# Bias table, value layout, decay rows and masked products of a hybrid attention/SSD layer rearranged

## The chip, the cores and the metric

One NeuronCore of a Trainium2 chip runs the whole layer as one program. The metric is the device time of an execution in microseconds (us), from the first to the last instruction of the core and what lies around it. The engines are TensorE (PE, with its weight loads as PEld), VectorE (DVE), ScalarE (ACT), GpSimd (POOL) and SyncE (SP). SP issues most of the DMAs, POOL some. Each engine, and each DMA-issuing queue, takes its instructions in order.

## The reference

The layer normalizes and modulates 1024 latent tokens and 256 context tokens of width 1024, projects them, and sends the columns to two groups of heads: eight heads of 2-D neighbourhood attention (a 16 x 64 grid, windows of 8 x 16, with all context keys in the same softmax) and eight heads of a bidirectional Mamba-2 (SSD) scan. An output projection, a gated MLP with a depthwise convolution, and a last RMSNorm follow. The scan in chunks of 128 tokens, for one direction, is

```python
cum = jnp.cumsum(dtc * a.reshape(g, e), axis=2)
seg = cum[:, :, :, None] - cum[:, :, None, :]
decay = jnp.exp(jnp.where(lower, seg, -jnp.inf))
cb = jnp.einsum("bcign,bcjgn->bcijg", cc, bc)
m = cb[..., None] * decay * dtc[:, :, None]
y_diag = jnp.einsum("bcijge,bcjgep->bcigep", m, xc)
...
y = y_f + flip(y_b) + d_skip[:, None] * xs
y = y.reshape(bsz, l, SSD_WIDTH) * jax.nn.silu(z)
```

and a row of the attention adds `rpb` at the window's offsets to the scores, and excludes keys outside the window. All is float32.

## The kernel before, in words

The program runs in stages on one core: norms and modulation; the q/k projections with rotary embedding (lines 278 to 308); the v projection (310 to 328); the SSD inputs with their convolution (508 to 539); the z projection (565 to 579); attention with the rest of the SSD beside it (596 to 781); the output projection; the MLP. Matmuls of the projections are made in three products of high and low parts. q, k, v, z and the summed decay exponents (`cum_d`) go through DRAM scratch tensors and are read back in the layout of the next stage.

**Values.** The v projection runs in two halves `b` of 256 columns. Each half has five units of two token blocks (ten blocks of 128 tokens, the last two context), evacuated into the one buffer of `vt` (L315). Its latent tokens are stored in `v_d` by column blocks `cb` and grid-row parity `r` (L323 to 327), eight stores, and the context in one (L328). `load_v(hp)` (L592) reads one head pair's 18 tiles back, in runs of 128 floats.

**SSD.** `ssd_steps` (L424) is a generator. Its steps are: the two initial states, seven steps of the backward state, then six steps for each of the eight chunks (`ssd_chunk`, L434). They are numbered 0 to 5 here. Step 0 multiplies C and B (`cb`), masks the product for both directions on DVE (`cbm`, L441), loads the decay rows `seg` of both directions, broadcast to 128 partitions, with two DMAs of 512 KB (L446), and subtracts each token's own sum on POOL (L447). Step 1 takes the minimum on DVE and the exp on ACT. Step 2 weights the masks with `dt`: the forward direction on DVE into `mt0`, the backward one on POOL into the buffer of `seg1` (L457), then POOL adds both (L459) and DVE multiplies by the decay (L460). Step 3 makes the products on TensorE (and advances the forward state), steps 4 and 5 gather the parts, multiply with silu(z), and sum the squares on ACT. The pool `sw` has one buffer of each tile.

**Who drives the generator.** The last two units of the SSD inputs take two steps each, the eight z units one each (L577), and each attention step `n` one (L779). Chunk 0 so reaches step 3 in the z stage; its steps 4 and 5 fall on n = 0 and 1, and chunk c (1 to 7) on n = 6c - 4 to 6c + 1. From n = 44 on the generator `out_steps` follows.

**Attention.** 64 steps, each for 128 queries of one head, in groups of eight (one head pair and half of the rows; four column blocks `cb`, two heads `j`). `attn_score` (L616) makes the scores in PSUM, DVE adds the bias table and finds the maximum (L638), ACT takes the exp (L639); `attn_turn`, two steps later, transposes on TensorE and copies on ACT (L650); `attn_out`, three steps later, multiplies with v. The tables, 24 in all, live in two buffers `tabt` (L599 to 608): table m + 1 is loaded at the first use of table m. The zero columns between a table's halves, for the context keys, are set once by POOL. Table 0 is loaded after the z stage, as `at`, the pool that holds `tabt` and `vp`, lies where the z stage's operands were.

**Order.** The program is written in this order, but within it the framework's planner sets the order of instructions of each engine and queue by modelled times, so a load can stand on SP ahead of, or behind, its place in the source. `reuse_waits="tile"` means that a new tile waits for the last use of the tiles whose memory it takes.

Of the kernel before, what the change touches and what calls it, by code (L numbers as in the profile page):

```python
# [17 lines left out]
P = 128  # L18
# [18 lines left out]
def hymba(ctx: ExitStack, tc: tile.TileContext, A):  # L37
# [23 lines left out]
    v_d = dram.tile([18, P, 512], FP, name="v_d")  # L61
# [180 lines left out]
    with ExitStack() as p1:  # L242
# [67 lines left out]
        for b in range(2):  # L310
# [11 lines left out]
            fs = slice(256 * b, 256 * b + 256)  # L322
            for cb in range(4):  # L323
                win = v_d[4 * cb:4 * cb + 4, :, fs].rearrange("g (i r c) f -> r c (g i) f", i=2, r=2)
                for r in range(2):
                    p0 = 64 * r + CB0[cb]
                    sp.dma_start(win[r], vt[p0:p0 + 32, 0:8])
            sp.dma_start(v_d[16:18, :, fs].rearrange("t p f -> p t f"), vt[:, 8:10])  # L328
# [94 lines left out]

    def ssd_steps():  # L424
        init_state(0, hf[0])
        init_state(1, yz[:, 7])
        yield
        for c in range(7, 0, -1):
            advance(1, c, yz[:, c], yz[:, c - 1])
            yield  # L430
        for c in range(8):
            yield from ssd_chunk(c)

    def ssd_chunk(c):  # L434
# [7 lines left out]
        seg = []  # L442
        for d in range(2):
            sg = sw.tile([P, 8, P], FP, tag=f"seg{d}", name=f"seg{d}_{c}")
            r0 = d * 64 + c * 8
            sp.dma_start(sg, cum_d[r0:r0 + 8].partition_broadcast(P))  # L446
            pool.tensor_tensor(sg, sg, cum[:, d, c][:, :, None].to_broadcast([P, 8, P]), OP.subtract)  # L447
            seg.append(sg)
        yield
        dve.tensor_tensor(seg[0], seg[0], seg[1], OP.min)  # L450
        act.activation(seg[0], seg[0], AF.Exp)
        yield
        mt = [sw.tile([P, 8, P], FP, tag="mt0", name=f"mt_{c}"), seg[1]]
        for d in range(2):
            for g in range(2):
                hs4 = slice(4 * g, 4 * g + 4)
                (pool if d else dve).tensor_tensor(mt[d][:, hs4], cbm[:, d, g][:, None, :].to_broadcast([P, 4, P]),  # L457
                                  dtv[:, c, 8 * d + 4 * g:8 * d + 4 * g + 4][:, :, None].to_broadcast([P, 4, P]), OP.mult)
        pool.tensor_tensor(mt[0], mt[0], mt[1], OP.add)  # L459
# [13 lines left out]
        sp.dma_start(yz[:, c], z_d[sl])  # L473
        ya = sw.tile([P, 512], FP, tag="ya", name=f"ya{c}")
# [4 lines left out]
        dve.tensor_tensor(v8(yb), v8(yo[:, 1]), bc64(ecum[:, 1, c]), OP.mult)  # L479
# [722 lines left out]
```

## Time and profile before

| | us |
|---|---|
| median of 3 runs (1397.27 to 1399.0) | 1398.22 |
| the profiled execution | 1403.42 |
| its span, first to last instruction | 1401.7 |

| engine | busy us | share of the span | instructions |
|---|---|---|---|
| PE | 1332.7 | 95% | 7539 |
| DVE | 858.5 | 61% | 1345 |
| ACT | 625.8 | 45% | 1049 |
| POOL | 303.2 | 22% | 295 |

A busy PE is not a PE at its peak: matmuls are pipelined and their ends are modelled. The idle time of an engine counts only where another waits for it. In the rows below, a row of a timeline gives the start and the duration in us, engine, line, operation, tile written and tiles read, shape, and in brackets how long the engine was idle before and what ended that. A row of groups ends with the count, the busy time in us, the mean of one in ns, and the idle time before them with its releasers. A row of windows gives the stretch (A:B), its length, the busy time of PE, PEld, DVE, ACT and POOL with the instructions of each, the granted clock, the DMA share and GB/s. [...]

### The profile page before, as it was taken

To read this page: it belongs to the slowest core of one execution; us is meant where nothing else is said; L and a number is where in the kernel's file an instruction comes from. 1 tells how busy PE (TensorE), PEld (TensorE's weight loads), DVE (VectorE), ACT (ScalarE), POOL (GpSimd) and SP (SyncE) were. 2 spreads that over 40 slices of the span, in tenths; PEclk is the share of its full clock that TensorE was granted. 3 is DMA by queue.
4 is the path that set the end of the run, shared out by engine and by line. 5 is a ranking of instruction groups with operands and counts; after the bars stand their busy time and mean duration, and the time that the engine had idled before them with its cause. 6 is when DMAs were issued, how large, how long until landed. Compare 5 with 4: busy or idle time off the path is not lost.

```text
span 1401.7 us, 20013 instructions
## 1 busy us (share of the span) xinstructions
PE 1332.7 (95%) x7539; PEld 1120.1 (80%) x7539; DVE 858.5 (61%) x1345; ACT 625.8 (45%) x1049; POOL 303.2 (22%) x295
## 2 busy tenths in 40 slices
PE   4999999999899999999989999999999999999996
PEld 2788998889877887777886888888888877887985
DVE  5684246742367766548877555666556584668664
ACT  5441224332155558536556444454445453455441
POOL 0010000024667752000222222221222102110120
PEclk9999999999999999999999999999999999999998
DMA  9564675521697687333857677766677677686782
GB/s 370 215 166 121 164 239 198 183 91 60 191 253 195 201 229 252 112 136 120 188 129 186 158 177 168 166 157 159 144 174 175 178 261 188 174 240 169 193 210 74
DMA packets 118160, 251.02 MB, mean 179 GB/s; under 512 B 11944, under 2 KB 37288, under 8 KB 116784
## 3 DMA queue, kind: packets, MB, share of 16 engines
q1 hardware_dynamic: 92576, 197.58, 43.9%
q0 software_dynamic: 25488, 52.18, 19.9%
q8 instruction: 59, 0.97, 0.3%
q14 instruction: 37, 0.30, 0.1%
HBM read 212.16 MB, written 37.55 MB: 178 GB/s over the span
## 4 chain that ended last, share of the span: by engine, by line
PE 77%; DMA 8%; DVE 5%; ACT 4%; POOL 3%; issue 3%; SPq 0%; DVEq 0%; POOLq 0%; ACTq 0%
PE u L871 27%; PE pd L90 10%; PE fu_qk L90 6%; PE fu_x L90 6%; PE tu_v L90 4%; PE oc L90 3%; PE tu_z L90 2%; PE pm L1037 2%; PE av L666 2%; DMA seg<-cum_d 2%; PE os L90 2%; PE oa L90 1%; PE pt L648 1%; PE fu_c L90 1%; DMA as<-in_w_up 1%
## 5 line engine op out<-in xcount | busy, mean ns | idle before, releaser
L871 PE MATMUL u<-op,whu 128*128 128x512 f32 (+1 forms) x760 | 227.0, 382 | 4.5 <-ACT yz L889 2.8
L871 PEld LDWEIGHTS u<-op,whu 128*128 128x128 f32 x760 | 139.4, 189 | 36.0 <-ACT yz L889 3.7
L871 PE MATMUL u<-op,wlu 128*128 128x512 f32 (+1 forms) x380 | 144.0, 380 | 0.0
L844 POOL DMA_DIRECT2D as<-in_w_up x69 | 65.9, 984 | 354.8 <-DMA as<-in_w_up 145.7
L863 ACT ACTIVATE whu<-as 128x512 fp32r<-128x512 f32 x115 | 67.6, 625 | 166.7 <-PE u L871 158.8
L871 PE MATMUL u<-opx,whu 128*128 128x512 f32 (+1 forms) x384 | 111.2, 381 | 4.1 <-ACT whu L863 3.6
L864 DVE TENSOR_TENSOR wlu<-as,whu 128x512 fp32r<-128x512 f32 x115 | 75.9, 685 | 24.7 <-ACT whu L863 24.6
L871 PEld LDWEIGHTS u<-opx,whu 128*128 128x128 f32 x384 | 70.5, 190 | 20.2 <-ACT whu L863 5.2
L90 PE MATMUL pd<-opx,wh_dn 128*128 128x512 f32 x256 | 81.5, 399 | 3.4 <-ACT wh_dn L79 3.3
L871 PEld LDWEIGHTS u<-op,wlu 128*128 128x128 f32 x380 | 71.7, 189 | 15.0
L894 DVE TENSOR_TENSOR xa<-u,yz 128x512 f32<-128x512 f32 (+1 forms) x24 | 15.5, 645 | 94.1 <-PE u L871 94.1
L871 PE MATMUL u<-opx,wlu 128*128 128x512 f32 (+1 forms) x192 | 72.0, 378 | 0.0
L639 ACT ACTIVATE pr<-pr,mx 128x640 f32<-128x640 f32 x64 | 52.8, 825 | 40.1 <-DVE mx L638 40.0
L638 DVE CUSTOM_DVE_ANT_0 pr<-s,tabt 128x640 f32<-128x640 f32 x64 | 51.9, 817 | 21.3 <-PE s L628 15.4
L666 PE MATMUL av<-pts,vp 128*64 128x128 f32 x640 | 56.6, 289 | 5.0 <-ACT pts L650 5.0
L90 PEld LDWEIGHTS pd<-opx,wh_dn 128*128 128x128 f32 x256 | 47.7, 189 | 16.7 <-ACT wh_dn L79 5.4
L851 POOL DMA_DIRECT2D yz<-in_w_up x46 | 52.2, 1158 | 33.9 <-ACT yz L850 30.4
L650 ACT ACTIVATE pts<-pt 128x640 f32<-128x640 f32 x64 | 43.9, 695 | 33.1 <-PE pt L648 20.7
L871 PE MATMUL u<-opz,whu 128*128 128x512 f32 (+1 forms) x192 | 56.3, 376 | 1.2 <-ACT yz L886 1.2
L666 PEld LDWEIGHTS av<-pts,vp 128*64 128x64 f32 x640 | 41.5, 142 | 17.8 <-ACT pts L650 8.6
L648 PE MATMUL pt<-cst,pr 128*128 128x128 f32 x320 | 49.2, 285 | 5.9 <-ACT pr L639 3.2
L627 PE MATMUL s<-k,q 128*128 128x384 f32 x128 | 49.8, 409 | 1.5 <-DVE mx L638 1.3
(641 smaller groups left out, 3571.1 us busy)
## 6 DMA issues: line engine op xcount, KB each, us to landing
as<-in_w_up SPq DMA_DIRECT2D x69, 256.0 KB, 4.0
as<-in_w_up POOLq DMA_DIRECT2D x69, 256.0 KB, 3.7
yz<-in_ada_wt SPq DMA_DIRECT2D x32, 512.0 KB, 4.4
ws_dn<-in_w_down SPq DMA_DIRECT2D x32, 448.0 KB, 4.2
as<-in_w_up SPq DMA_DIRECT2D x23, 512.0 KB, 5.5
yz<-in_w_up POOLq DMA_DIRECT2D x46, 256.0 KB, 5.6
g_d<-xa POOLq DMA_DIRECT2D x22, 512.0 KB, 4.8
tabt<-in_tab SPq DMA_DIRECT2D x48, 192.0 KB, 4.7
```

The source lines that it names most:

```text
L90: pe.matmul(out[:, t0:t1], st(a, k), mv(b, k, t0, t1), start=k == 0 and p == 0, stop=k == kend - 1 and p == 2, **kw)
L627: pe.matmul(ps[:, loc0:loc0 + 384], qs, kl, start=a == 0, stop=a == 1)
L638: dve.tensor_tensor_reduce(pr, ps[:, lo:lo + 640], tabt[m % 2][:, 384 * j:384 * j + 640], -1.0, BIG, OP.add, OP.min, mx)
L639: act.activation(pr, pr, AF.Exp, bias=mx, scale=-1.0, accum_out=sm[:, n % 8:n % 8 + 1])
L648: pe.transpose(pt[:, i * P:(i + 1) * P], pr[:, i * P:(i + 1) * P], ident)
L650: act.activation(pts, pt[:, 0:640], AF.Copy)
L666: pe.matmul(av[64 * j:64 * j + 64, cb], vt, pp[j][:, i * P:(i + 1) * P], start=i == 0, stop=i == 4, skip_group_check=True)
L844: pool.dma_start(t, d, accum_op=OP.add)
L851: pool.dma_start(t, d, accum_op=OP.add)
L863: act.activation(h, src, AF.Copy)
L864: dve.tensor_tensor(l, src, f32(h), OP.subtract)
L871: mm = pe.matmul(ps[:, t0:t1], aops[n, o][a][:, k], bops[o][b][:, k, t0:t1], start=first and o < 5 and (t0 == 0 or n == 2), stop=end, skip ...
```

## The change

- **First table.** Table 0 goes into the first 1024 columns of `ctm`, a tile of the context tokens that is free once the initial states are made; its loads and the zeroing stand in the first step of the second half of the z stage. The two `tabt` buffers take the other tables in turn.
- **Values.** `v_d` is laid out by head pair and partition, so that a head pair's load has one run of 18 x 128 floats in each partition. The stores of a half become 32 of 64 KB for the latent tokens and two for the context; the 32 of the second half are issued by POOL.
- **Decay rows.** Even chunks keep their two decay tiles in `sw`, odd chunks have theirs in a second pool `swx`, opened beside `at` when the z stage is over. The load for chunk c + 1 stands at step 0 of chunk c, its subtraction at step 5 of chunk c (chunk 0: load ahead of the initial states, subtraction at its own step 0; chunk 1: load at step 4 of chunk 0).
- **Masked products.** ACT multiplies the backward mask with `dt`, head by head, into `mt0`; DVE then multiplies the forward mask with `dt` and adds, head by head, in place. POOL's products and its sum are gone.
- **Moved.** The square of a chunk stands at step 1 of the next one, the last one after all chunks; POOL's sum of `yb` and `xd` moves from step 5 to step 4.

```diff
-    v_d = dram.tile([18, P, 512], FP, name="v_d")
+    v_d = dram.tile([4, P, 18, P], FP, name="v_d")
...
-            fs = slice(256 * b, 256 * b + 256)
-            for cb in range(4):
-                win = v_d[4 * cb:4 * cb + 4, :, fs].rearrange("g (i r c) f -> r c (g i) f", i=2, r=2)
-                for r in range(2):
-                    p0 = 64 * r + CB0[cb]
-                    sp.dma_start(win[r], vt[p0:p0 + 32, 0:8])
-            sp.dma_start(v_d[16:18, :, fs].rearrange("t p f -> p t f"), vt[:, 8:10])
+            for hp in range(2):
+                v = vt[:, :, P * hp:P * hp + P]
+                vd = v_d[2 * b + hp]
+                for cb in range(4):
+                    win = vd[:, 4 * cb:4 * cb + 4].rearrange("(i r c) g f -> r i c g f", i=2, r=2)
+                    for r in range(2):
+                        p0 = 64 * r + CB0[cb]
+                        for i in range(2):
+                            (pool if b else sp).dma_start(win[r, i], v[p0:p0 + 32, i:8:2])
+                sp.dma_start(vd[:, 16:18], v[:, 8:10])
...
+    def seg_load(c):
+        segs[c] = []
+        for d in range(2):
+            sg = swx[c % 2].tile([P, 8, P], FP, tag=f"seg{d}", name=f"seg{d}_{c}")
+            r0 = d * 64 + c * 8
+            sp.dma_start(sg, cum_d[r0:r0 + 8].partition_broadcast(P))
+            segs[c].append(sg)
+
+    def seg_less(c):
+        for d in range(2):
+            pool.tensor_tensor(segs[c][d], segs[c][d], cum[:, d, c][:, :, None].to_broadcast([P, 8, P]), OP.subtract)
+
+    def square(c):
+        yb = sw.tile([P, 512], FP, tag="yb", name=f"sq{c}")
+        act.activation(yb, yz[:, c], AF.Square, accum_out=ssq[:, c:c + 1])
...
     def ssd_steps():
+        seg_load(0)
         init_state(0, hf[0])
...
         for c in range(8):
             yield from ssd_chunk(c)
+        square(7)
...
-        seg = []
-        for d in range(2):
-            sg = sw.tile([P, 8, P], FP, tag=f"seg{d}", name=f"seg{d}_{c}")
-            r0 = d * 64 + c * 8
-            sp.dma_start(sg, cum_d[r0:r0 + 8].partition_broadcast(P))
-            pool.tensor_tensor(sg, sg, cum[:, d, c][:, :, None].to_broadcast([P, 8, P]), OP.subtract)
-            seg.append(sg)
+        if c == 0:
+            seg_less(0)
+        elif c < 7:
+            seg_load(c + 1)
+        seg = segs.pop(c)
         yield
+        if c:
+            square(c - 1)
         dve.tensor_tensor(seg[0], seg[0], seg[1], OP.min)
         act.activation(seg[0], seg[0], AF.Exp)
         yield
-        mt = [sw.tile([P, 8, P], FP, tag="mt0", name=f"mt_{c}"), seg[1]]
-        for d in range(2):
-            for g in range(2):
-                hs4 = slice(4 * g, 4 * g + 4)
-                (pool if d else dve).tensor_tensor(mt[d][:, hs4], cbm[:, d, g][:, None, :].to_broadcast([P, 4, P]),
-                                  dtv[:, c, 8 * d + 4 * g:8 * d + 4 * g + 4][:, :, None].to_broadcast([P, 4, P]), OP.mult)
-        pool.tensor_tensor(mt[0], mt[0], mt[1], OP.add)
+        mt = [sw.tile([P, 8, P], FP, tag="mt0", name=f"mt_{c}")]
+        for h in range(8):
+            act.activation(mt[0][:, h], cbm[:, 1, h // 4], AF.Copy, scale=dtv[:, c, 8 + h:9 + h])
+        for h in range(8):
+            dve.scalar_tensor_tensor(mt[0][:, h], cbm[:, 0, h // 4], dtv[:, c, h:h + 1], mt[0][:, h], OP.mult, OP.add)
         dve.tensor_tensor(mt[0], mt[0], seg[0], OP.mult)
...
         sp.dma_start(yz[:, c], z_d[sl])
+        if c == 0:
+            seg_load(1)
...
+        pool.tensor_tensor(yb, yb, xd, OP.add)
         yield
+        if c < 7:
+            seg_less(c + 1)
         dve.tensor_tensor(ya, ya, yd, OP.add)
-        pool.tensor_tensor(yb, yb, xd, OP.add)
         dve.tensor_tensor(ya, ya, yb, OP.add)
         pool.tensor_tensor(yz[:, c], ya, yz[:, c], OP.mult)
-        act.activation(yb, yz[:, c], AF.Square, accum_out=ssq[:, c:c + 1])
...
+    tabt = [ctm]
+    table = lambda m: tabt[1 + m % 2 if m else 0]
...
                 if b and not qks:
+                    pool.memset(ctm[:, 384:640], 0.0)
+                    for j in range(2):
+                        load_tab(0, j)
                     load_qk(0)
...
-        sp.dma_start(vps[hp], v_d[:, :, P * hp:P * hp + P].rearrange("t p f -> p t f"))
+        sp.dma_start(vps[hp], v_d[hp])
```

## Rows read from the trace of the kernel before

**Rows 1.** Chain of waits from 350 to 640 us: shares by line

```profile
by line: PE av L666 10.0%; DMA seg<-cum_d 9.7%; PE os L90 8.5%; PE oa L90 7.0%; PE pt L648 6.8%; PE s L627 5.5%; issue 5.4%; POOL mt L459 3.2%; PE s L628 2.8%; POOL seg L447 2.6%; DMA tabt<-in_tab 2.6%; DVE pr L638 2.5%; PE tu_z L90 2.4%; P
```

**Rows 2.** Windows over chunks 1 to 7: stretch, length, busy by engine, clock, DMA

```profile
377.96:401.99 24.03, 19.34 (x132) 16.44 (x133) 13.43 (x29) 10.17 (x22) 13.90 (x10) 0.86 1.04 292
401.99:422.76 20.77, 18.48 (x152) 15.57 (x152) 17.41 (x25) 11.43 (x23) 16.62 (x11) 1.00 0.74 208
422.76:440.33 17.57, 17.25 (x140) 14.35 (x139) 14.38 (x27) 11.82 (x24) 10.08 (x8) 1.00 0.92 241
440.33:465.43 25.10, 22.65 (x165) 19.50 (x164) 15.66 (x26) 10.32 (x22) 19.43 (x14) 0.86 0.74 232
465.43:483.90 18.47, 18.47 (x155) 15.81 (x154) 15.21 (x27) 11.93 (x25) 13.54 (x9) 1.00 0.42 118
483.90:508.99 25.09, 22.39 (x160) 19.41 (x159) 14.53 (x26) 11.08 (x22) 16.07 (x11) 0.86 0.90 242
508.99:527.38 18.39, 17.67 (x148) 14.88 (x147) 13.81 (x26) 11.47 (x25) 8.29 (x6) 1.00 0.78 198
```

**Rows 3.** Timeline of DVE: the minimum of the decay tiles, chunks 2 to 7

```profile
402.30 2.29 DVE L450 TENSOR_TENSOR seg<-seg,seg 128x1024 f32<-128x1024 f32 x1
...
420.24 2.28 DVE L450 TENSOR_TENSOR seg<-seg,seg 128x1024 f32<-128x1024 f32 x1 [1.31 <-POOL seg L447]
...
445.80 2.05 DVE L450 TENSOR_TENSOR seg<-seg,seg 128x1024 f32<-128x1024 f32 x1 [3.73 <-POOL seg L447]
...
470.30 1.23 DVE L450 TENSOR_TENSOR seg<-seg,seg 128x1024 f32<-128x1024 f32 x1 [0.56 <-POOL seg L447]
...
492.21 1.22 DVE L450 TENSOR_TENSOR seg<-seg,seg 128x1024 f32<-128x1024 f32 x1 [2.68 <-POOL seg L447]
...
513.39 1.21 DVE L450 TENSOR_TENSOR seg<-seg,seg 128x1024 f32<-128x1024 f32 x1
```

**Rows 4.** Chain of waits at chunk 4, in order of time: start, length, what

```profile
430.58 2.38 POOL mt L459
432.98 7.90 DMA seg<-cum_d
441.01 1.90 POOL seg L447
```

**Rows 5.** Timeline of DVE at the start of attention: the first score operation

```profile
383.19 0.82 DVE L638 CUSTOM_DVE_ANT_0 pr<-s,tabt 128x640 f32<-128x640 f32 x1 [2.63 <-DMA tabt<-in_tab]
```

**Rows 6.** Groups by line and shape: masked products, and the nearest small operations

```profile
L457 POOL TENSOR_TENSOR seg<-cbm,dtv 128x512 f32<-128x512 f32 x16 | 20.1, 1273 | 7.4 <-DVE seg L450 3.7 <-DVE cbm L441 3.6
L459 POOL TENSOR_TENSOR mt<-mt,seg 128x1024 f32<-128x1024 f32 x8 | 19.3, 2410 | 1.2 <-DVE mt L457 0.7
...
L457 DVE TENSOR_TENSOR mt<-cbm,dtv 128x512 f32<-128x512 f32 x12 | 13.1, 1131 | 0.0
...
L356 DVE SCALAR_TENSOR_TENSOR dta<-dtv,na 128x160 f32<-128x160 f32 x1 | 0.3, 326 | 0.0
...
L347 ACT ACTIVATE dt<-dt 128x160 f32<-128x160 f32 x1 | 0.3, 338 | 0.0
...
L639 ACT ACTIVATE pr<-pr,mx 128x640 f32<-128x640 f32 x36 | 29.7, 825 | 21.6 <-DVE mx L638 21.6
L650 ACT ACTIVATE pts<-pt 128x640 f32<-128x640 f32 x37 | 25.5, 695 | 20.8 <-PE pt L648 15.8 <-PE av L666 4.9
```

**Rows 7.** v: stores on SP; the projection in the chain; DMA issues; POOL's own

```profile
166.73 6.44 SPq L327 DMA_DIRECT2D v_d<-vt  x8
...
142.76 58.29 PE tu_v L90 x480
...
v_d<-vt SPq DMA_DIRECT2D x18, 256.0 KB, 4.0
vp<-v_d SPq DMA_DIRECT2D x4, 1152.0 KB, 9.4
...
L905 POOL DMA_DIRECT2D g_d<-xa x22 | 15.4, 698 | 79.1 <-DVE xa L904 79.1
```

More of the change, by code (lines that the diff above doesn't have):

```diff
@@ L422, in advance @@
         dve.tensor_tensor(dst, tmp, ps, OP.add)
+    segs = {}
+    def seg_load(c):
[11 more added lines that the diff above has]
+        act.activation(yb, yz[:, c], AF.Square, accum_out=ssq[:, c:c + 1])
     def ssd_steps():
+        seg_load(0)
         init_state(0, hf[0])
@@ L518, in hymba @@
             sw = open_sw()
+            swx = [sw]
             hf = [sw.tile([P, 512], FP, name=f"hf{i}") for i in range(2)]
@@ L541, in hymba, with load_tab @@
     qks = {}
+    tabt = [ctm]
+    table = lambda m: tabt[1 + m % 2 if m else 0]
+    def load_tab(m, j):
+        if m < 24:
+            c = 640 * j
+            sp.dma_start(table(m)[:, c:c + 384], A["tab"][2 * (m // 6) + j, m % 6])
     def load_qk(g):
@@ L585, in hymba @@
     at = pb.enter_context(tc.tile_pool(name="at", reuse_waits="tile", bufs=2))
+    sx = ExitStack()
+    swx.append(sx.enter_context(tc.tile_pool(name="swx", reuse_waits="tile", bufs=1)))
     bigp = pb.enter_context(tc.tile_pool(name="bigp", reuse_waits="tile", bufs=3, space=PSUM))
@@ L593, in load_v @@
         vps[hp] = at.tile([P, 18, P], FP, tag="vp", name=f"vp{hp}", bufs=2)
-        sp.dma_start(vps[hp], v_d[:, :, P * hp:P * hp + P].rearrange("t p f -> p t f"))
+        sp.dma_start(vps[hp], v_d[hp])
+    tabt += [at.tile([P, 1024], FP, name=f"tabt{i}", bufs=1) for i in range(2)]
+    for t in tabt[1:]:
+        pool.memset(t[:, 384:640], 0.0)
     load_v(0)
@@ L598, in hymba @@
     sp.dma_start(selh, A["selh"])
-    tabt = []
-    for i in range(2):
-        t = at.tile([P, 1024], FP, name=f"tabt{i}", bufs=1)
-        pool.memset(t[:, 384:640], 0.0)
-        tabt.append(t)
-    def load_tab(m, j):
-        if m < 24:
-            c = 640 * j
-            sp.dma_start(tabt[m % 2][:, c:c + 384], A["tab"][2 * (m // 6) + j, m % 6])
-    for j in range(2):
-        load_tab(0, j)
     steps = [(hp, rb, cb, j) for hp in range(4) for rb in range(2) for cb in range(4) for j in range(2)]
@@ L637, in attn_score @@
         mx = at.tile([P, 1], FP, tag="mx", name=f"mx{n}", bufs=4)
-        dve.tensor_tensor_reduce(pr, ps[:, lo:lo + 640], tabt[m % 2][:, 384 * j:384 * j + 640], -1.0, BIG, OP.add, OP.min, mx)
+        dve.tensor_tensor_reduce(pr, ps[:, lo:lo + 640], table(m)[:, 384 * j:384 * j + 640], -1.0, BIG, OP.add, OP.min, mx)
         act.activation(pr, pr, AF.Exp, bias=mx, scale=-1.0, accum_out=sm[:, n % 8:n % 8 + 1])
@@ L708, in out_steps @@
         nonlocal xa
+        sx.close()
         sd.close()
```

## The prediction

> **What bounds the kernel now.** I first read the chain of waits over the stretch that the diff touches, from the end of the z projection to the first output projection. TensorE's lines fill most of it, but one transfer stands second: the load of the decay rows, `seg<-cum_d`, with 9.7% [rows 1]. TensorE should never wait for a 512 KB load whose contents were known long before, so the next view cuts the stretch into the seven SSD chunks that run beside the attention scores. Each chunk is six generator steps, one step per attention step, so the cuts stand at the first score matmul of every sixth attention step. The chunks take 24.03, 20.77, 17.57, 25.10, 18.47, 25.09 and 18.39 us, 149.42 us in all, for the same work but for what falls on a cut [rows 2]. Three are slow, three quick, and chunk 2 lies between. The slow ones (1, 4, 6) are also those whose granted clock is 0.86 instead of 1.00.
>
> What tells slow from quick is on DVE: before the minimum of a chunk's two decay tiles it sat idle for POOL's subtraction, not at all in chunk 2, 1.31 us in 3, 3.73 in 4, 0.56 in 5, 2.68 in 6, not at all in 7 [rows 3]. So a wait over 2.5 us makes a slow chunk, one up to 1.3 us a quick one. The size fits: against the mean of the three quick ones, (17.57 + 18.47 + 18.39) / 3 = 18.14 us, chunks 4 and 6 take 7.0 us more, of which the waits are 3.7 and 2.7, and a clock of 0.86 over 25.1 us loses (1 - 0.86) x 25.1 = 3.5 us of full clock: 7.2 and 6.2. The low clock comes in no chunk without such a wait (chunk 1 has the start's, below). Chunk 2's 2.6 us have another cause: the same minimum takes 1.2 us in some chunks and 2.3 in others [rows 3], and chunk 2 has DVE busy for 17.41 us against 13.8 to 15.2 in the quick ones, with POOL at its densest (16.62 of 20.77, 80%) [rows 2]; I read this as DVE slowed by POOL's work.
>
> Why the rows come late shows in the chain at chunk 4: POOL's sum of the masked products ends, the load runs 7.90 us, then the subtraction starts [rows 4]. The products of chunk c are built in the buffer of its second decay tile, and there is one buffer of each tile, so chunk c+1's rows cannot be loaded before chunk c's products are finished. Products, load, subtraction, minimum, exp, products form a loop through four engines, and behind the minimum DVE's other work (the sums that free the one PSUM bank of the SSD products) waits in order.
>
> The start has a stall of its own: DVE's first score operation waits 2.63 us for the first bias table and starts at 383.19 [rows 5], behind the z stage.
>
> **The change part by part.** *Decay rows a chunk ahead* (second pair of buffers, load at step 0 of the chunk before, subtraction at its step 5). It removes nothing but the dependence: 14 loads and 14 subtractions are still made. A load now has five steps, 5 x 17.57 / 6 = 14.6 us at the quickest chunk's pace, against 7.90 us for the late one. With no wait left, and the 5 us that POOL loses below gone from beside DVE, I give chunks 2 to 7 the 18.14 us of the quick ones: 6 x 18.14 = 108.9 against 125.4 now, **-16.5 us**. On SP the load moves ahead of the tables and q/k loads of five steps; its buffer was freed four steps before, so it holds nothing up. What is late next is DVE, busy 14 to 15 us of a quick chunk [rows 2].
>
> *First table in a free buffer.* The two loads move into the z stage, where TensorE is fed by other data, so they cost nothing: no engine waits for them before the z stage has ended. The 2.63 us wait goes. Chunk 1 is 24.03 - 18.14 = 5.9 us over a quick one; part of the rest is the low clock, which should not come if the pause is shorter. Against it, chunk 1's own rows now go to memory that is free only when the z stage has ended, and land later than before; their slack is the products of that chunk. Bounds: 0 and 5.9; I take **-4 us**.
>
> *Products head by head.* Removed per chunk: on POOL two products of 1.27 us and a sum of 2.41 us, 4.95 us; on DVE two products of 1.13 us, 2.26 us. Added: eight ACTIVATEs of 128x128 and eight SCALAR_TENSOR_TENSORs of 128x128 [rows 6]. Neither shape, with a per-partition scalar from SBUF, is in the trace. For DVE the nearest is 128x160 from SBUF in 326 ns; 8 x 0.326 = 2.6 us is an upper end, as the new ones are 32 columns shorter, and I take them as equal to the 2.26 that goes. For ACT the nearest is 128x160 in 338 ns, 8 x 0.338 = 2.7 us; the score exp, with a scalar from SBUF, takes 825 ns at 640 columns against 695 for the copy without, and with those 130 ns on each the upper end is 3.7 us. I take 2.7, the row of nearly the same shape. ACT is busy 11.5 to 11.9 us of the quick chunks [rows 2], so about 14.4 of 18.1. I take the pair at **0**: the cover is ACT's idle 6 us per chunk. If it covers nothing, 7 x 2.7 = 18.9 us come back; on the other side, a freer POOL, and DVE beside it, could give up to (18.14 - 17.1) x 6 = 6 us more (17.1 is worked out below).
>
> [...] The trace's own nearest row is the 338 ns for 160 columns [rows 6]. [...]
>
> *Values in long runs.* The load of v has 1152 KB, landing in 9.4 us [rows 7]; with one run per partition I expect less, but it is taken at 0, as the first product that needs it comes behind the scores. The stores come in smaller pieces: per half 32 of 64 KB and two for the context instead of 8 of 256 KB and one. Before, eight took 6.44 us to issue, 0.81 us each, on SP; the new ones, a quarter of the bytes, lie between 0.2 (by bytes) and 0.81 (by count). At 0.4 us (twice the price by bytes), 34 take 13.6 us. The first half's end at 166.7 + 13.6 + 4.0 us of landing = 184 [rows 7]. The tile `vt` has one buffer, so the next half's first copy, due when its unit ends at 142.76 + 6 x 5.83 = 177.7 [rows 7], waits some 6 us; three PSUM buffers of 5.83 us hide that until about 190. So **0**; at 0.81 us it would be 34 x 0.81 = 27.5, end at 198, 8 us lost. The second half's 32 go on POOL at some 0.70 us (as `g_d<-xa`), 22 us, with nothing else to do there.
>
> *Moved pieces.* The squares go one step later, the sum of yb and xd one earlier, in the same number: 0.
>
> **Sum.** -16.5 - 4 = -20.5 us. The profiled execution took 1403.42 us, 1.7 more than its span and 5.2 more than the median of the runs; 1403.4 - 20.5 = 1382.9 there, 1377.7 beside the median of 1398.22: **1378 us**.
>
> **The rivals.**
> - *Transfers bind next* (part of the gain). The DMA share times the length of the seven chunks sums to 25.0 + 15.4 + 16.2 + 18.6 + 7.8 + 22.6 + 14.3 = 119.9 us, 17.1 us a chunk [rows 2]. In 129 us that is a share of 0.93. Landings would grow and the tables, loaded two steps ahead of use at each group of eight, would hold DVE as the first one does now. At 2 us, once per chunk for five chunks, 10 us come back: 1388. For it: the 1.04 in chunk 1. Against it: chunk 3 was the quickest of all at 0.92. Chance 0.18.
> - *More than the quick chunks show.* POOL had 5 us more to do in these as well. With all seven at the transfers' 17.1 us, 149.4 - 119.9 = 29.5 us go: 1369. Against it: TensorE is already busy 17.25 of chunk 3's 17.57. Chance 0.15.
> - *The rows are not early after all.* SP is in order, and a load behind a table that waits for its buffer is no earlier than before; then only the start gains: 1394. Five steps speak against it. Chance 0.07.
> - *ScalarE blocks: slower.* The eight ACTIVATEs wait for the masked products of DVE at the head of ACT's queue, and behind them stand the exp and the copy that the next transposes and products on TensorE need. It decides from 20.5 / 7 = 2.9 us lost per chunk. With the pieces at their upper end of 3.7 us, nothing hidden, 3.7 x 7 = 25.9 us stand against 20.5: 1398.2 + 5.4 = 1403.6. [...] Against it: the step between the masking and the weighting, and ACT's 6 idle us in 18. Chance 0.08.
>
> **How the numbers follow.** The forecast has 0.52. Its own range, from a start that gives 0 to 6 us and chunks of 17.6 to 18.5, is 1373 to 1385. To hold 8 in 10 the range takes in both part gains, the floor of 17.1 with some more at the start, and on the other side the third rival, or ACTIVATEs of which 16 of the 18.9 us show (-20.5 + 16 = -4.5): 1364 to 1394. A measurement of this kernel tells 0.2%, 2.8 us, from nothing. Faster: 0.52 + 0.18 + 0.15 and a little of the third rival, 0.86. Slower: the fourth, 0.08. The same: 0.06.
>
> **What would show it.** Right: POOL's subtractions wait for no load but chunk 1's; all chunks from 2 on between 17 and 19 us with clock 1.00; no wait of DVE for the first table; TensorE without a gap around 172 to 200 us. Wrong: chunks near 20 us with TensorE waiting for `pts` or `pr` from ACT, or DVE waiting for tables, or the first decay minimum still held by POOL.

## The result, and the profile after

The changed kernel takes 1418.9 us in the median of four runs (1416.78 to 1426.0) where the kernel before, in the same series, takes 1398.61 (1397.27 to 1401.38): a ratio of **1.014 [1.0108, 1.0172]**, slower, where 1378 and faster was forecast. The profiled execution took 1416.78 us with a span of 1415.0, 13.3 more than the span before. It is the quickest of its four, and the one before (1403.42) was slower than all runs of its series, so the traces show less than the 20 us between the medians. The medians of the kernel before drift by some 4 us between series, so each run below is given as a ratio to the runs of the kernel before in its own series; 0.1% is 1.4 us.

Where the 13.3 us lie, from the starts and ends of TensorE's stages in both traces: +1.6 before the v projection (there is no change there), **+5.5** between the v and the z projection, 0 in the z stage, **+4.8** from the start of attention to the end of chunk 1, -1.5 in chunks 2 to 7, **+4.9** in the steps n = 44 to 55, -1.9 behind them. The first and the last of these lie within what single traces scatter: over all the traces of the kernels below, the stretch before the v projection, which no part touches, takes 142.2 to 144.4 us, and what comes behind n = 55 takes 834.5 to 850.5.

The windows over chunks 1 to 7, cut as in [rows 2]:

```profile
384.67:413.88 29.21, 22.52 (x130) 18.07 (x128) 20.69 (x35) 14.03 (x33) 13.19 (x9) 0.77 0.99 285
413.88:434.90 21.02, 19.86 (x161) 16.60 (x160) 19.15 (x33) 14.17 (x30) 14.50 (x10) 1.00 0.74 212
434.90:456.36 21.46, 16.80 (x136) 13.91 (x136) 15.20 (x29) 13.03 (x30) 8.51 (x7) 1.00 0.88 245
456.36:477.30 20.94, 20.94 (x163) 18.55 (x163) 15.39 (x34) 12.24 (x30) 9.51 (x8) 0.92 0.66 220
477.30:500.15 22.85, 20.71 (x157) 16.88 (x156) 18.00 (x34) 14.85 (x33) 7.58 (x6) 0.95 0.45 127
500.15:521.24 21.09, 20.39 (x156) 17.75 (x155) 13.55 (x32) 13.47 (x30) 5.50 (x4) 0.90 0.66 180
521.24:537.76 16.52, 16.25 (x135) 13.38 (x134) 11.36 (x29) 10.94 (x26) 2.57 (x2) 1.00 0.85 194
```

The slow and quick chunks of [rows 2] have become six of 20.9 us and more, with one quick one at the end. POOL, 80% busy in the densest chunk before, is nearly idle at the end; DVE and ScalarE have more to do. Chunk 1 is the longest of all.

The groups by line and shape over 350 to 545 us that answer to [rows 6] and [rows 3]:

```profile
L480 DVE SCALAR_TENSOR_TENSOR mt<-cbm,dtv,mt 128x128 f32<-128x128 f32 x64 | 31.3, 543 | 1.4 <-ACT mt L478 1.4
L439 POOL TENSOR_TENSOR seg<-seg,cum 128x1024 f32<-128x1024 f32 x13 | 25.2, 1940 | 35.4 <-DMA seg<-cum_d 27.5 <-DMA tabt<-in_tab 7.3 <-ACT mt L478 0.7
L478 ACT ACTIVATE mt<-cbm,dtv 128x128 f32<-128x128 f32 x64 | 19.8, 391 | 5.0 <-DVE cbm L464 5.0
L473 DVE TENSOR_TENSOR seg<-seg,seg 128x1024 f32<-128x1024 f32 x7 | 12.4, 1765 | 10.7 <-POOL seg L439 10.7
```

POOL still waits 27.5 us for decay rows, and the minimum (L473) 10.7 us for POOL. The head-by-head operation of DVE has a mean of 543 ns. What hides in that mean is seen in chunk 1, first on DVE, then on POOL, and last a chunk with POOL out of the way:

```profile
384.28 0.82 DVE L665 CUSTOM_DVE_ANT_0 pr<-s,ctm 128x640 f32<-128x640 f32 x1
...
389.84 0.82 DVE L665 CUSTOM_DVE_ANT_0 pr<-s,tabt 128x640 f32<-128x640 f32 x1 [2.21 <-DMA tabt<-in_tab]
...
391.19 8.13 DVE L480 SCALAR_TENSOR_TENSOR mt<-cbm,dtv,mt 128x128 f32<-128x128 f32 x8
...
509.31 2.17 DVE L480 SCALAR_TENSOR_TENSOR mt<-cbm,dtv,mt 128x128 f32<-128x128 f32 x8
```

```profile
391.18 1.90 POOL L439 TENSOR_TENSOR seg<-seg,cum 128x1024 f32<-128x1024 f32 x1 [5.51 <-DMA seg<-cum_d]
393.03 1.09 POOL L405 TENSOR_TENSOR xws<-xtm,wend 128x512 f32<-128x512 f32 x1
394.08 1.35 POOL L509 TENSOR_TENSOR yz<-ya,yz 128x512 f32<-128x512 f32 x1
395.39 1.09 POOL L424 TENSOR_TENSOR adv<-hf,dec 128x512 f32<-128x512 f32 x1
396.44 1.94 POOL L439 TENSOR_TENSOR seg<-seg,cum 128x1024 f32<-128x1024 f32 x1
```

The first score operation no longer waits for a table (384.28, against the 2.63 us of [rows 5]), but the third, the first that uses the second table, now waits 2.21 us (389.84). And the eight operations at 391.19 take 8.13 us instead of 2.17: the first five last 2.04, 1.13, 1.38, 1.13 and 1.98 us and end one by one with POOL's five instructions, the last three take 0.34 each. POOL comes at that moment because chunk 1's rows have come late. In the seven chunks the 56 operations fill 28.9 us where 7 x 2.17 = 15.2 would do.

Between the projections, TensorE's first transposes, then DVE's convolution steps before (L494 and L495) and after (L518 and L519):

```profile
231.19 1.97 PE L525 MATMUL tp_x<-cst,xfm 128*128 128x128 f32 x8 [3.65 <-ACT xfm L520]
```

```profile
213.54 1.28 DVE L494 SCALAR_TENSOR_TENSOR xfm<-fu_x,vec,xfm 128x1023 f32<-128x1023 f32 x1 [2.72 <-ACT xfm L493]
214.86 1.28 DVE L495 SCALAR_TENSOR_TENSOR xfm<-fu_x,vec,xfm 128x1023 f32<-128x1023 f32 x1
```

```profile
215.13 1.28 DVE L518 SCALAR_TENSOR_TENSOR xfm<-fu_x,vec,xfm 128x1023 f32<-128x1023 f32 x1 [2.72 <-ACT xfm L517]
226.23 1.28 DVE L518 SCALAR_TENSOR_TENSOR xfm<-fu_x,vec,xfm 128x1023 f32<-128x1023 f32 x1 [9.82 <-ACT xfm L517]
227.43 1.27 DVE L519 SCALAR_TENSOR_TENSOR xfm<-fu_x,vec,xfm 128x1023 f32<-128x1023 f32 x1
```

The two lines are the two steps of one unit. Before, a unit's two stood together. Now L518 of the second unit (226.23) is queued ahead of L519 of the first (227.43) and waits 9.82 us for its operand; TensorE, with nothing else in its order, waits 3.65 us for the first unit, and the clock granted to it falls to 0.88 of full speed over 216 to 232 us (1.00 before).

### The profile page after: what moved, and what is told of

Its sections match the earlier page's. It is cut to its first block, busy times and chain, and to the rows that moved or that the text cites. A ratio compares the mean times of both kernels' runs of the same rounds, so it can differ in the third digit from the quotient of the medians.

```text
span 1415.0 us, 20159 instructions
## 1 busy us (share of the span) xinstructions
PE 1341.0 (95%) x7539; PEld 1124.6 (79%) x7539; DVE 870.5 (62%) x1393; ACT 647.5 (46%) x1115; POOL 282.3 (20%) x304
## 4 chain that ended last, share of the span: by engine, by line
PE 70%; DMA 12%; DVE 7%; issue 5%; ACT 4%; POOL 1%; SPq 0%; DVEq 0%; POOLq 0%; ACTq 0%
PE u L899 23%; PE pd L90 7%; PE fu_qk L90 7%; PE fu_x L90 6%; PE tu_v L90 4%; PE oc L90 3%; PE tu_z L90 2%; PE av L693 2%; DMA as<-in_w_up 2%; PE os L90 2%; PE pm L1065 1%; PE oa L90 1%; DMA tabt<-in_tab 1%; DVE mt L480 1%; PE pt L675 1%
## 5 line engine op out<-in xcount | busy, mean ns | idle before, releaser
L665 DVE CUSTOM_DVE_ANT_0 pr<-s,tabt 128x640 f32<-128x640 f32 x62 | 50.6, 819 | 22.3 <-PE s L655 14.8
```

The source lines that it names most:

```text
L665: dve.tensor_tensor_reduce(pr, ps[:, lo:lo + 640], table(m)[:, 384 * j:384 * j + 640], -1.0, BIG, OP.add, OP.min, mx)
```

## The experiments

### The four parts, each undone and each alone

Undone in the changed kernel (the old text of that part put back, as below, the diffs cut to their core), and alone in the kernel before (the same lines the other way round):

```diff
# undo_products, only_products
-        for h in range(8):
-            act.activation(mt[0][:, h], cbm[:, 1, h // 4], AF.Copy, scale=dtv[:, c, 8 + h:9 + h])
...
+        pool.tensor_tensor(mt[0], mt[0], mt[1], OP.add)
# undo_values, only_values
-    v_d = dram.tile([4, P, 18, P], FP, name="v_d")
+    v_d = dram.tile([18, P, 512], FP, name="v_d")
# undo_rows, only_rows (with the squares and the sum of yb and xd)
-            sg = swx[c % 2].tile([P, 8, P], FP, tag=f"seg{d}", name=f"seg{d}_{c}")
+            sg = sw.tile([P, 8, P], FP, tag=f"seg{d}", name=f"seg{d}_{c}")
# undo_table, only_table
-    tabt = [ctm]
+    tabt = []
```

Expected, undone ("port theory" is the author's name for a guess, that DVE's operations lose time to POOL's beside them; the runs show times, not a port):

> The changed kernel with the old masked products (two on DVE, two and the sum on POOL), the rest as changed. Port theory: in the changed kernel 16 of the 64 head-by-head DVE operations run beside a POOL instruction and take 1147 instead of 342 ns, 12.9 us in all, mostly in front of TensorE; with the old products these go, POOL's 5 us a chunk come back beside other work: 1404 to 1410 us, chunk 1 about 24 us instead of 29.2. Rows theory: the chunks are slow as the decay rows come late all the same (POOL's subtraction waits 20.0 us for loads): the old products change little, 1416 to 1422, chunks 2 to 6 stay at 20.6 us and over.

> The changed kernel with the old layout, stores and loads of v. Order theory: the 66 small stores move the modelled times by which the order of the instructions is set, and that order holds TensorE by 5.5 us at 216 to 232 us; with the old stores TensorE has no gap there and the time falls to 1412 to 1415. Rival: the stretch at 216 to 232 belongs to DVE work beside POOL, whatever the v stores: 1418 to 1420, gap still there.

> The changed kernel with the decay rows as before (one pair of buffers, load at step 0, subtraction behind it, the squares and the sum of yb and xd at their old places). Rows theory: loading ahead brings nothing, as its loads wait for memory or stand behind others on SP; undoing it gives 1417 to 1422. Port theory: the subtraction, put at step 5, now falls beside the head-by-head products of the next chunk's step 2; put back, it stands ahead of the minimum, on which the products' step follows, and the products run alone: 1408 to 1413. If loading ahead did bring what was predicted, 1430 to 1436.

> The changed kernel with the first table loaded after the z stage into its own buffer. Prediction's step: the first score operation of DVE waits 2.6 us again, and with what follows 4 us are lost: 1422 to 1424. Rival: the start is held by chunk 1's products beside POOL in any case, so the wait is hidden there: 1417 to 1420.

Expected, alone:

> The kernel before with the masked products head by head on ScalarE and VectorE, and nothing else changed. Port theory: about half the head-by-head operations of DVE fall beside POOL's subtraction or other sums and the kernel becomes slower by itself: ratio 1.004 to 1.010. Prediction's step (products at 0, POOL freed): 0.995 to 1.001, since POOL's sum no longer holds the decay buffer.

> The kernel before with the new layout, stores and loads of v, and nothing else changed. Undoing it in the changed kernel took the ratio from 1.014 to 1.0059. Order theory (the stores move the order of later instructions by the modelled times): the loss shows here too, TensorE waits at 216 to 232 us, ratio 1.004 to 1.008. Rival (the loss needs the other parts, as the stores only shift when things meet): 0.998 to 1.002.

> The kernel before with the first table in the free tile, and nothing else changed. Prediction's step: the 2.63 us wait of DVE's first score operation goes, ratio 0.997 to 0.999. What undoing it in the changed kernel showed (1.0098 against 1.014): the loads or the zeroing in the z stage cost more than the wait: 1.002 to 1.005.

> The kernel before with the decay rows a chunk ahead (and the squares and the sum of yb and xd moved), the old products, v and first table. Prediction's step: -16.5 us, ratio 0.988; POOL's subtractions wait for no load from chunk 2 on, and chunks 2 to 7 take 18 us. Rows theory (the loads come late all the same): 0.998 to 1.003, with the subtraction waiting 15 us or more for loads. Port theory (rows early pays where the products don't lose to POOL): 0.988 to 0.995.

> The kernel before with the first table in the free tile, as before, in more rounds. Prediction's step of -4 us: ratio 0.996 to 0.998. Rival (an effect of the runs): 0.999 to 1.001.

Measured:

| part | alone | the change without it (all four: 1.014) |
|---|---|---|
| products head by head | 1.0091 [1.006, 1.0122] | 1.0048 [1.0021, 1.0075] |
| values in long runs | 1.0055 [1.0022, 1.0087] | 1.0059 [1.0036, 1.0083] |
| decay rows ahead | 1.000 [0.9976, 1.0024] | 1.0162 [1.0132, 1.0191] |
| first table | 0.9973 [0.995, 0.9996]; again, five rounds: 0.9985 [0.9955, 1.0014] | 1.0098 [1.0081, 1.0116] |

Without the products chunk 1 falls from 29.2 to 16.7 us, and the seven chunks from 153.1 to 143.7; without the values TensorE's transposes start with no pause, and more comes back (0.81%) than the expected range allowed (1412 to 1415 us, 0.3 to 0.5%); without the rows nothing is gained. Alone, the products cost 0.9%, the values 0.55%, the table brings 0.15 to 0.27, and the rows change nothing, as the second of the three theories on them had it: POOL's subtraction waits 15.1 us for loads. Alone they add up to +1.19%, 16.6 us, and 1.40% (1.08 to 1.72) was measured; undone one by one they come to 1.93%, with the noise of the 1.40 four times in it. So the parts add, as far as this can tell. The table's two columns don't fit together: undoing it should not have helped, and that expectation failed on both sides, though the two intervals (up to 1.0116, from 1.0108) just overlap. A lead, not a cause: n = 44 to 55 take 33.3 us in the kernel before and 33.3 to 35.4 wherever table or products are missing, and 38.2, 38.7 and 40.4 in the three that have both (the change, and the change without values or without rows); at that place the change has DVE waiting 2.1 us for one table, and its chain of waits runs through the landing of another, 12.20 us.

### Products: the port theory or ScalarE

```diff
# act_and_wide_dve: ScalarE's pieces stay, DVE's eight become three
+        for g in range(2):
...
+            dve.tensor_tensor(mt[0][:, hs4], cbm[:, 0, g][:, None, :].to_broadcast([P, 4, P]),
...
+        dve.tensor_tensor(mt[0], mt[0], mt[1], OP.add)
# dve_beside_pool: a tail behind the last output, DVE's batch once alone, once beside POOL
...
+    for i in range(32):
+        pool.tensor_tensor(wide(3), wide(3), wide(2), OP.add)
```

> The kernel before with a tail that computes nothing of use: on DVE eight head-by-head operations of 128x128, two 128x512 products, two 128x1024 minima, four 128x512 additions with one operand in PSUM, four one-operand 128x512 additions, once alone and once beside a chain of 33 additions of 128x1024 on POOL; eight 128x128 ACTIVATEs with a scale column beside the same. Port theory: alone the head-by-head operation takes 0.34 us, beside POOL it ends with POOL's instruction, up to 1.9 us each, and so does every two-operand operation from SBUF; the additions with PSUM and the ACTIVATEs do not change. Rival (only sharing of bandwidth): all take at most twice as long, 0.7 us for the head-by-head operation.

> The kernel before with the backward products head by head on ScalarE, as in the change, but the forward ones as two 128x512 products on DVE and the sum as one 128x1024 addition on DVE: three DVE instructions a chunk in place of eight, POOL's three gone as in the change. Port theory (each DVE instruction beside POOL can lose one POOL instruction): loss well below that of the head-by-head form, ratio 0.998 to 1.004. ScalarE theory (its eight pieces and its place in the chain cost): as with the head-by-head form, 1.007 to 1.012.

The groups of the tail, first alone (1403 to 1416 us), then beside POOL (1417 to 1460):

```profile
L1129 DVE TENSOR_TENSOR yz<-yz,probe 128x512 f32<-128x512 f32 x4 | 2.7, 687 | 0.2
L1127 DVE TENSOR_TENSOR yz<-yz 128x1024 f32<-128x1024 f32 x2 | 2.5, 1226 | 0.1
L1120 DVE SCALAR_TENSOR_TENSOR yz<-yz,vec 128x128 f32<-128x128 f32 x8 | 2.2, 348 | 0.0
L1131 DVE TENSOR_SCALAR yz<-yz 128x512 f32<-128x512 f32 x4 | 1.7, 427 | 0.1
L1123 DVE TENSOR_TENSOR yz<-yz,vec 128x512 f32<-128x512 f32 x2 | 1.3, 686 | 0.0
```

```profile
L1141 POOL TENSOR_TENSOR yz<-yz 128x1024 f32<-128x1024 f32 x17 | 42.7, 2512 | 1.3
L1120 DVE SCALAR_TENSOR_TENSOR yz<-yz,vec 128x128 f32<-128x128 f32 x8 | 19.2, 2470 | 0.0
L1131 DVE TENSOR_SCALAR yz<-yz 128x512 f32<-128x512 f32 x4 | 9.3, 2333 | 0.1
L1127 DVE TENSOR_TENSOR yz<-yz 128x1024 f32<-128x1024 f32 x2 | 6.5, 3247 | 0.1
L1129 DVE TENSOR_TENSOR yz<-yz,probe 128x512 f32<-128x512 f32 x4 | 2.7, 686 | 0.1
L1145 ACT ACTIVATE yz<-yz,vec 128x128 f32<-128x128 f32 x4 | 1.6, 402 | 67.0 <-DVE yz L1131 66.9
```

Beside a busy POOL the eight 128x128 operations took 2470 ns each instead of 348, about one POOL addition (2512); the rival, shared bandwidth, allowed twice the time. The two 128x512 products took 1750 ns in the mean, against 686 alone, so not both took a whole addition. The addition that reads one operand from PSUM (`probe`) is untouched (686 ns, 687 alone), and ScalarE's piece takes 402 ns, near the 391 in the changed kernel. With three wide DVE instructions a chunk the kernel takes **1.0034 [1.0007, 1.006]**, 8 us less than head by head and within what the port theory expected. Its groups over 376 to 545 us, behind those of only_products:

```profile
L457 DVE SCALAR_TENSOR_TENSOR mt<-cbm,dtv,mt 128x128 f32<-128x128 f32 x56 | 25.2, 500 | 0.0
```

```profile
L458 DVE TENSOR_TENSOR mt<-cbm,dtv 128x512 f32<-128x512 f32 x14 | 9.8, 742 | 0.0
L460 DVE TENSOR_TENSOR mt<-mt,seg 128x1024 f32<-128x1024 f32 x7 | 8.9, 1273 | 0.7 <-ACT seg L455 0.7
```

Against their times alone (7 x 2.17 us, 686 ns, 1226 ns) the head-by-head form takes 10 us more and the wide one 1.1. So the small pieces make most of the loss, and time lost beside POOL fits it in size. That this is all of their price is not shown: over the seven chunks DVE also waits 14.5 us for subtractions with the eight pieces, 10.2 with the wide form and 8.3 before, and whether these waits only follow from later products was not separated. The 0.34% that stays, with ScalarE's pieces and the addition that moved from POOL to DVE, was not taken apart further.

### Values: the order or the stores

```diff
# values_dve_pinned (values alone, and one edge of order on DVE)
+        with tc.issue_after(x0_last[0]) if key == "x1" else ExitStack():
             dve.scalar_tensor_tensor(out[:, 1:], ps[:, :n - 1], cw[:, 0:1], out[:, 1:], OP.mult, OP.add)
```

> The kernel before with the new layout, stores and loads of v, and one thing more: the first convolution step of the second SSD input unit on DVE is put behind the last one of the first unit, as in the kernel before. Order theory: TensorE's pause of 3.66 us before the first transposes and the low clock behind it go, of the 5.4 us lost between the v projection and the z projection 4 to 5 come back, ratio 0.999 to 1.002. Rival (the stores cost by their number or their transfers): 1.004 to 1.008 as without the pin.

The same rows in this kernel:

```profile
226.97 1.09 PE L509 MATMUL tp_x<-cst,xfm 128*128 128x128 f32 x8 [1.09 <-ACT xfm L502]
```

From the end of the v projection to the start of the z projection it is 116.5 us before, 122.0 with the values alone, 117.8 with the edge: 4.2 of the 5.5 us come back, and the eight transposes take 1.09 us instead of the 1.97 with the values alone. The ratio is 1.0035 [1.0006, 1.0064], between the two expectations; its interval overlaps that without the edge. In the stage the loss is the order's. What else the values cost over the whole, if anything, stays open.

### Decay rows: wait, transfer, queue, or place

```diff
# no_row_loads: kernel before, loads only for chunk 0, exp with scale=1e-3
+            if not c:
...
+                sp.dma_start(seg[d], cum_d[d * 64:d * 64 + 8].partition_broadcast(P))
# loads_nobody_waits: the same, with the loads put back into tiles that nothing reads
+                sp.dma_start(swx[0].tile([P, 8, P], FP, tag=f"segx{d}", name=f"segx{d}_{c}"),
...
# rows_table_min_pinned: rows and table, the minimum queued behind the chunk before
+        with tc.issue_after(muls[-1]) if muls else ExitStack():
             dve.tensor_tensor(seg[0], seg[0], seg[1], OP.min)
# rows_on_act_queue, rows_on_pool_queue (pool.dma_start): rows and table, another queue
-            sp.dma_start(sg, cum_d[r0:r0 + 8].partition_broadcast(P))
+            act.dma_start(sg, cum_d[r0:r0 + 8].partition_broadcast(P))
# rows_pool_tables_act: rows on POOL's queue, and
-            sp.dma_start(table(m)[:, c:c + 384], A["tab"][2 * (m // 6) + j, m % 6])
+            (act if m else sp).dma_start(table(m)[:, c:c + 384], A["tab"][2 * (m // 6) + j, m % 6])
```

> The kernel before, leaving out the loads of the decay rows for chunks 1 to 7: the subtraction, minimum and exp work in place on what the tiles hold (the exp with a scale of 0.001 that keeps the numbers small), so only the transfer's time and its place on SP and the DMA engines are gone. Prediction's step: the transfer in front of the subtraction is what makes slow chunks, so without it chunks 2 to 7 take some 18 us each, ratio 0.986 to 0.990. Order theory (the chunk's pace is set by the orders of five in-order engines, in which the rows are only one of several late operands): 0.995 to 1.000, chunks still between 17 and 25 us.

> The run without the loads of the decay rows for chunks 1 to 7, with as many loads of the same size put back at the same place, into two tiles that nothing reads (left out as there: the rows themselves). If it is the wait of the subtraction that costs, the ratio stays at 0.9905 (0.987 to 0.994) and the chunks at 19.4 us. If it is SP's queue or the DMA engines, the tables or q and k come later and it returns to 0.997 to 1.002.

> The kernel before with the first table in the free tile and the decay rows a chunk ahead, and the minimum of a chunk put on DVE behind the multiplication that ends the masked products of the chunk before (in the run with the rows alone, the minimum stood ahead of it in DVE's order from chunk 3 on, and DVE waited there for POOL's subtraction). Order theory: the waits of DVE for the subtraction (5.3 us in that run) go, ratio 0.990 to 0.996. Rival (the rows are no cost at any place): the table's gain alone, 0.996 to 0.999.

> First table in the free tile, decay rows a chunk ahead, their loads issued by ScalarE's queue in place of SP's; old products, old v. Queue theory (loads of rows and tables stand behind each other's waits on SP): waits of DVE for tables (7.8 and 10.6 us in the two runs with rows ahead on SP) go, ratio 0.985 to 0.993. DMA engine theory (the bytes cost): tables late all the same, 0.996 to 1.002.

> The same with the loads of the rows issued by POOL's queue, so that they stand right behind POOL's own work and no wait for a table is ahead of them. Queue theory: 0.985 to 0.995, less than on ScalarE's queue by what POOL needs to issue them (some 0.7 us each, beside DVE). DMA engine theory: 0.997 to 1.003.

> First table in the free tile, decay rows a chunk ahead on POOL's queue, and the other tables issued by ScalarE's queue in place of SP's. Queue theory: the 8.4 us that DVE waits for tables go, chunks 2 and 3 fall to 20 us, ratio 0.989 to 0.994. Rival (ScalarE, in order, now holds its exp behind the tables' buffers, or the transfers are late on any queue): 0.996 to 1.002.

Measured, with the lengths of the chunks in the profiled execution (us; two executions of the table alone gave 61.6 and 61.2, 85.9 and 82.2, so some 4 us are no difference):

| kernel | ratio | chunks 1 to 3 | chunks 4 to 7 |
|---|---|---|---|
| before | 1 | 62.4 | 87.1 |
| no_row_loads | 0.9905 [0.9873, 0.9937] | 59.8 | 76.4 |
| loads_nobody_waits | 0.9915 [0.9887, 0.9943] | 62.5 | 77.0 |
| only_rows | 1.000 [0.9976, 1.0024] | **70.2** | **78.2** |
| rows_table_min_pinned | 0.9997 [0.9965, 1.0028] | 69.3 | 85.8 |
| rows_on_act_queue | 1.000 [0.9973, 1.0028] | 62.1 | 83.5 |
| rows_on_pool_queue | 0.9977 [0.9942, 1.0012] | 66.8 | 77.6 |
| rows_pool_tables_act | 1.0029 [1.0001, 1.0057] | 63.3 | 87.2 |

Without the loads 13.3 us go, near the 16.5 forecast. With the same bytes loaded and not waited for, nearly all of it stays, although DVE then waits 6.0 us for tables (2.3 without the loads): it is the wait that costs, not the transfers or their issue on SP. These loads don't wait at the head of SP for products to end; what such a wait holds up behind it was not tested. With the rows alone, chunks 4 to 7 gain 8.8 us, close to what they gain without loads; but with rows and products as before the traces have 80.6 us (the values alone) to 87.1 there, so part of it may be scatter. Chunks 1 to 3 lose 7.9. It begins at chunk 1. Its loads on SP, its two subtractions on POOL and the multiplication that ends its products on DVE, before:

```profile
366.08 1.59 SPq L446 DMA_DIRECT2D seg<-cum_d  x2
...
370.00 1.90 POOL L447 TENSOR_TENSOR seg<-seg,cum 128x1024 f32<-128x1024 f32 x1 [3.94 <-DMA seg<-cum_d]
...
391.30 1.22 DVE L460 TENSOR_TENSOR mt<-mt,seg 128x1024 f32<-128x1024 f32 x1
```

and in only_rows:

```profile
380.90 1.45 SPq L431 DMA_DIRECT2D seg<-cum_d  x2
...
386.49 1.90 POOL L436 TENSOR_TENSOR seg<-seg,cum 128x1024 f32<-128x1024 f32 x1
...
402.00 1.22 DVE L480 TENSOR_TENSOR mt<-mt,seg 128x1024 f32<-128x1024 f32 x1
```

The odd chunks' buffers lie where the z stage's operands were. Before, chunk 1 had the buffers of chunk 0 and was loaded at 366; now chunk 2's loads stand there, a whole chunk before they are needed, and chunk 1's go out 14.8 us later. The z stage's memory explains some 6 of these: TensorE ends the stage at 372, and on ScalarE's queue the same loads go out then:

```profile
372.06 0.86 ACTq L431 DMA_DIRECT2D seg<-cum_d  x2
```

The other 8.8 us are SP's order: there the last store of `z_d` (5.50 us from 373.02), `selh`, three table loads and one of `yz` stand ahead. With the rows alone, chunk 1's products are done 10.7 us later, and the time is lost two chunks on: chunk 1 takes 24.07 us and chunk 2 19.86, no more than before, chunk 3 26.30 instead of 17.57. Its window, and the waits of POOL, DVE and TensorE that lead to it:

```profile
421.50:447.80 26.30, 22.33 (x159) 18.11 (x157) 16.75 (x28) 11.69 (x22) 17.61 (x12) 0.87 0.88 234
```

```profile
408.78 1.90 POOL L436 TENSOR_TENSOR seg<-seg,cum 128x1024 f32<-128x1024 f32 x1 [9.08 <-DMA seg<-cum_d]
```

```profile
432.36 2.30 DVE L470 TENSOR_TENSOR seg<-seg,seg 128x1024 f32<-128x1024 f32 x1 [3.33 <-POOL seg L436]
```

```profile
436.12 1.33 PE L674 MATMUL pt<-cst,pr 128*128 128x128 f32 x5 [3.25 <-DVE mx L664]
```

Chunk 3's rows go into chunk 1's buffers, at 401.6 and 403.4. Their subtraction stands ahead of chunk 2's products in POOL's order, so POOL idles 9.08 us for them, and chunk 2's products end at 422.4 instead of 413.5. Only as they end are chunk 4's rows loaded, and chunk 4's minimum stands ahead of chunk 3's products in DVE's order: DVE waits 3.33 us, TensorE 3.25, and the clock is 0.87. The lead that the source gives to a load is not the lead that the order gives it.

In the changed kernel chunk 1's rows are issued at 383.4 and 384.6 and the multiplication runs at 408.7.

The rest were misses, each with its cause not reached. Queueing the minimum later (with the first table beside it) took DVE's wait for subtractions from 5.3 us (only_rows) to 1.4, and its waits for tables rose from 7.8 to 10.6 (2.6 before). On ScalarE's queue, where chunk 1's rows are early, DVE waits 1.5 us for tables and chunks 1 to 3 lose nothing; but chunks 4 to 7 (83.5) lie within those 80.6 to 87.1, and the ratio is 1.000. So a late chunk 1 is not the whole of it. On POOL's queue POOL waits 1.0 us for rows in all, and chunks 4 to 7 are as quick as without loads; still the ratio is that of the table alone. There DVE waits for tables:

```profile
DVE pr L664 <- DMA tabt<-in_tab: 8.4, 2, 5.6
```

With the tables on ScalarE's queue those 8.4 us went, POOL's waits for rows came back (7.3 us), and the ratio is 1.0029: the gain that the queue theory expected (0.989 to 0.994) did not come, and what took it is open. What this points to, odd chunks in the early buffers and even ones from chunk 2 on in the late ones, was not run.

No run beats both kernels by much: among those that compute everything the first table alone (0.9973 and 0.9985) and the rows on POOL's queue with it (0.9977) are lowest, and only the first of the three has an interval that stays below 1.

## Why the prediction was wrong, step by step

- **Decay rows ahead, -16.5: measured 0.** The diagnosis stood: the wait for these rows is worth 13.3 us. The step that failed is "With no wait left". With the rows alone DVE still waits 5.3 us for subtractions (8.3 before) and 7.8 for tables (2.6 before): 13.1 us in place of 10.9. Two premises failed under it. "A load now has five steps" was read from the source; in the order, chunk 3's subtraction is begun as its load lands, 7.2 us after the issue, and stands ahead of chunk 2's products. And of the start it was said: "Against it, chunk 1's own rows now go to memory that is free only when the z stage has ended, and land later than before; their slack is the products of that chunk." That got no price of its own. The subtraction, minimum and exp also stand in that slack, chunk 1's products end 10.7 us late, and 7.9 us are lost by the end of chunk 3. Chunks 4 to 7 gained 8.8 of the 14.5 us that 18.14 a chunk would give. The trace that the 16.5 come from was also a long one: in the five traces with rows and products as before the seven chunks take 143.4 to 149.4 us, and 149.4 is its own. Why the rows bring nothing where chunk 1 comes earlier (1.000 on ScalarE's queue) stays open.
- **Products head by head, 0: measured +0.91%, 12.7 us.** The failed step is "I take them as equal to the 2.26 that goes". The size was right only undisturbed (2.17 us for eight), and the 2.26 that went was itself a price beside POOL: 1131 ns a product, where the tail has 686 alone. ScalarE's price was right: 391 ns a piece, against the 338 to 468 that the rows allowed. What was missed is that a 128x128 operation of DVE beside POOL can cost about a whole POOL instruction (2470 ns for 348 in the tail), so that eight in place of two offer four times the chances. The prediction had the sign of it, the minimum of 1.2 or 2.3 us in [rows 3], "DVE slowed by POOL's work", and used it only in favour of the change. Not every operation paid it: in the tail the additions with an operand in PSUM took 686 ns for 687 alone, while the one-operand additions from SBUF took 2333 for 427.
- **Values, 0: measured +0.55%, 7.7 us.** What was worked out held in its outcome: 34 stores on SP in 17.5 us (13.6 taken), the copy of the second half 12.7 us late and hidden (the projection takes 58.29 us as before), 32 on POOL at 560 ns (700 taken), the load landing in 7.6 us instead of 9.4. The failed step is "So **0**", a sum over the stores, their buffer and the load alone: the planner's order of work 30 us further on changed, and 5.5 us went there, of which one edge of order gave 4.2 back.
- **First table, -4: measured -3.8 and -2.1.** Right in size, alone, as far as the scatter lets one say: the second interval reaches past 1. Of the mechanism, "The 2.63 us wait goes" holds for the first score operation, but in both traces of the table alone (1.98 and 2.15 us), as in the change (2.21), the third one waits for the second table. In the whole change no gain is seen: without the table it was quicker, 1.0098.
- **Rivals.** The slower one was to come from ScalarE blocking at the head of its queue; ScalarE's wait for the masks was 5.0 us in all, and the loss came from DVE and from chunk 1. "The rows are not early after all" was right for chunk 1: SP's order makes 8.8 of its 14.8 us, though the load stands behind a store of `z_d` more than behind tables, and memory some 6. Of "Transfers bind next" the sign came, DVE waiting for tables (7.8 us with the rows alone); but with the same bytes loaded and 6.0 us of such waits, loads_nobody_waits kept the gain.
- **What would show it.** Named as right: POOL waiting for no load but chunk 1's, chunks of 17 to 19 us at full clock. Seen: 27.5 us of waiting and chunks of 21. Nothing in the list looked outside the stages that the diff touches.

## What to carry to other kernels

Before splitting a DVE operation into small ones, count the POOL instructions that run beside it: the price of each piece here was its own time or about theirs (348 or 2470 ns in the tail). When buffers are doubled in memory that opens late, look at who gets the late one and what stands ahead of its load in the queue; here it was the chunk needed first (giving it to the one needed last was not run). Look for the lead of a load in the order of the engines, and not in the source. And where a planner orders the program by modelled times, any change in number or kind of transfers can move work in stages that it does not touch: each part of a change is timed alone.

## What the runs showed of the hardware

In the tail DVE's 128x128 operations, with both tensor operands in SBUF, took about the time of one POOL addition each beside POOL, although seven times shorter alone (348 ns): eight in a row in 19.22 us, 2470 ns in the mean, where a POOL addition took 2512 (32 of them 80.21 us). The two-operand 128x512 addition with one operand in PSUM was free of this, 686 and 687 ns. The one-operand 128x512 addition from SBUF was not: 2333 ns beside POOL, 427 alone. Both read one operand from SBUF, so the number of SBUF operands does not tell them apart; what does was not tested.
